# A hybrid decoder layer on one Trainium2 core: the norm gains loaded by themselves, the first weights loaded over two queues and cast by VectorE, the first sums for the down weights put behind the first plain chunk, and cached keys loaded ahead of raw query weights

## The chip, the cores and the metric

The kernel runs on one core of a Trainium2 chip. The core has TensorE (PE, matrix products into PSUM), VectorE (DVE), ScalarE (ACT), GpSimd (POOL) and SyncE (SP, which here only issues DMAs); ACT and POOL issue DMAs as well. The metric is the device time of one execution in microseconds (us). Three runs of the kernel before took 1117.34, 1118.7 and 1119.95 us; their median, 1118.7 us, is the time before.

## What is computed

One layer for 512 prompt positions and 8 x 8 sample positions that use the same weights (576 columns in all), with model width 1024, feed-forward width 2816, and 256 memory tokens in 4 heads of 256:

```
def swiglu(x, w_gate, w_up, w_down):
    return (jax.nn.silu(x @ w_gate) * (x @ w_up)) @ w_down

def layer_forward(x, conv_buf, lru_h, pool_buf, mem_k, mem_v, pos0, p):
    x = x + 0.5 * swiglu(rmsnorm(x, p['ffn1_norm']), p['ffn1_w_gate'], p['ffn1_w_up'], p['ffn1_w_down'])
    h = rmsnorm(x, p['mix_norm'])
    proj = h @ p['w_in']
...
    x = x + jnp.concatenate([y_lru, y_pool], axis=-1) @ p['w_out']
    x = x + cross_attend(rmsnorm(x, p['xattn_norm']), mem_k, mem_v, p['xattn_wq'], p['xattn_wo'])
    x = x + 0.5 * swiglu(rmsnorm(x, p['ffn2_norm']), p['ffn2_w_gate'], p['ffn2_w_up'], p['ffn2_w_down'])
    return x, conv_buf, lru_h, pool_buf
```

`rmsnorm(x, g)` is x times the reciprocal root of its mean square plus 1e-6, times the gain g. A last rmsnorm follows the layer. The prompt attends over keys and values made from `mem_prompt`, the samples over cached ones.

## The kernel before

**Operands.** Everything is float32. An operand is split into a high part of type float32r and the float32r remainder (`split`, L186): ACT makes the high part (the cast of L192, or L196 where a scale is applied) and DVE subtracts it (L195, L197). A product of two operands is three matmuls: high x high, high x low, low x high. x lies in SBUF with the model width along 128 partitions in 8 blocks k = 0 to 7 and 576 columns, in two halves of 288.

**Feed-forward.** Both feed-forward blocks run through one function, `ffn` (FFN1 with `head` set, FFN2 without). The width 2816 is 22 chunks of 128. FFN1 does chunks 0, 1 and 2 plainly: gate and up, 8 blocks k of 6 matmul pairs. `std_out` (L410) scales them by the row factor, applies Silu and multiplies. The other chunks (f = 3 to 21 in FFN1, f = 2 to 21 in FFN2, 39 in all) use seven products of half size in place of eight, with the weights' sums E, F, G, H beside the blocks 11, 12 and 22. The loop L806 to L880 writes one chunk: products 11, E, (22 and the rest of the chunk before), F, G, 12, H; between them stand preparations of the next chunks' weights (`prepare_e`, `prepare_g`, `prepare_h`, `prepare_22`, `sum_eh`) and, by `fill`, steps of the down projection of earlier chunks. `sum_eh` (L450) adds two weight blocks on DVE (L453) and starts a POOL DMA that adds a third from memory (L456). `prepare_g` adds the others (L471, L472). `prepare_22` casts and splits block 22 (128x512): the cast to tile `wh` on ACT and its remainder `wl` on DVE. The copy `u` of the U product (L852) stands in program order just ahead of `prepare_22`.

**Down projection.** `quick` (L633) does four chunks at a time in the same seven-product form, on PSUM tiles dU, dC, dA and dD. Its weights come from raw tiles `td` and `t` (SP DMAs L594, L600), with sums on DVE (L612, L614, L615, L623) in `ensure` and splits to `dh` and `dl`. ACT scales results out of PSUM (`take`, L642); POOL DMAs add them onto x.

**Head.** ACT issues the load of all constants (`cst`, 99 columns, L108); DVE negates two gains (L127, `neg`); a dummy activation loads the Sqrt table (L135); PE runs six warm matmuls (L141). Then SP loads, for k = 0 to 7, x[k] (L707), and, for even k, two blocks each of the gate and up weights of chunk 0 (L710, `wr`). For each k ACT and DVE split x[k] with the negated gain into `n1h` and `n1l` (`HalfNorm.split`, L330), for even k the weights into `wh` and `wl`, and PE does chunk 0's 12 matmuls of this k. `sums(p)` (L332) makes sums of the normed x on ACT and DVE for the seven-product form (tiles `t_ph`, `t_pl`). The row factor of FFN1's norm (L735 to L745) comes from squares of a second, row-wise copy of x (`xs`, L740, L741), Sqrt (L742) and a few small DVE steps (L285 to L289); PE spreads it over the partitions (the moves, L758 to L761) and ACT copies it to `rstd_n` (L764). `std_out(0)` then reads it (L416).

**Queries.** In the cross-attention `query(p)`, p = 0 to 3, makes queries of a pair of blocks by the same seven products. `load_q` loads raw query weights (`q`, L1333), `prepare_q` makes sums of them (on POOL for p > 0: L1344 to L1350) and splits them. `load_keys` loads cached keys (`ck`, L1317) and `sample_scores` multiplies them with the samples' queries on PE (tile `ss`). Raw weights and keys share six buffers of 512 KB (the tag `wr`): a load waits on SP until its buffer is free, and the loads queued behind it wait with it.

**Order.** `mm` chains every matmul of the feed-forward and query phases to the one before, so PE's order is that of the program. The order of DVE, ACT, POOL and SP is made by a scheduler from the program order, the dependences and a few hand-set "after" edges (`after_`, L142: an order on one engine, no wait). The edges touched here are `first[0]`, behind which casts of weights are held (L192), `row_done`, the last step of the row factor, and `out_[0]`, the last copy out of PSUM in the chunk loop.

## Time and profile before

| what | value |
|---|---|
| median of three runs | 1118.7 us (1117.34 to 1119.95) |
| the profiled execution's own time | 1118.21 us |
| its span on the core | 1116.1 us |
| busy time, share of the span | PE 99%, DVE 79%, ACT 62%, POOL 19% |
| matmuls | 8396 |
| DMA | 181.19 MB, mean 162 GB/s |
| granted TensorE clock | 0.999 |

The span is the time from the core's first instruction to its last; 2.1 us of the execution lie outside it. A row of the timeline gives start, duration, engine, line, operation, output and inputs, how many equal instructions in a row it stands for, and in brackets how long the engine was idle before and what ended that. SPq and ACTq rows are DMA issues, and their duration runs from the first issue to the end of the last.

### The profile page before, as it was taken

What the parts mean: (1) busy time and instruction counts of PE and PEld (TensorE: products, weight loads), DVE (VectorE), ACT (ScalarE), POOL (GpSimd) and SP (SyncE); (2) the same over time, 40 slices, a digit from 0 to 9 for tenths busy, and PEclk for the clock granted to TensorE, in tenths of its full rate; (3) what the DMA queues carried; (4) which work ended last, traced back from release to release, by engine and by line L of the source; (5) the groups of instructions that cost most, each with busy time, mean ns of one, the idle gap of its engine ahead of it and who ended that gap; (6) DMA issues with size and microseconds to landing.
All of it is one profiled execution on the core that took longest, in us unless ns stands there. A gap on an engine that the chain in (4) does not pass through costs nothing.

```text
span 1116.1 us, 22006 instructions
## 1 busy us (share of the span) xinstructions
PE 1101.8 (99%) x8396; PEld 1081.6 (97%) x8396; DVE 882.5 (79%) x1580; ACT 689.2 (62%) x1293; POOL 212.5 (19%) x248
## 2 busy tenths in 40 slices
PE   8999999999999999999999999999999999999997
PEld 8999999999999999999988879999999999999997
DVE  7899888889866878979865666779888888787755
ACT  8566666676664645786743555446666666666554
POOL 0012222221221034422131000000222122222211
PEclk9999999999999999999999999999999999999999
DMA  9457777776766655577557952233786877877652
GB/s 313 127 131 178 157 153 169 169 169 149 170 138 144 188 158 130 125 210 169 158 179 275 323 204 83 76 99 82 161 184 149 187 171 159 188 158 169 134 122 85
DMA packets 95577, 181.19 MB, mean 162 GB/s; under 512 B 10032, under 2 KB 47920, under 8 KB 95344
## 3 DMA queue, kind: packets, MB, share of 16 engines
q1 hardware_dynamic: 61328, 125.73, 35.3%
q0 software_dynamic: 31472, 51.65, 28.3%
q10 hardware_dynamic: 2672, 2.41, 0.6%
q8 instruction: 65, 1.06, 0.4%
q14 instruction: 40, 0.33, 0.1%
HBM read 141.92 MB, written 13.20 MB: 139 GB/s over the span
## 4 chain that ended last, share of the span: by engine, by line
PE 92%; issue 3%; DMA 2%; DVE 1%; ACT 1%; POOL 0%; SPq 0%; POOLq 0%; DVEq 0%; ACTq 0%
PE pu L149 23%; PE pc L149 11%; PE dU L149 9%; PE pa L149 5%; PE xo L149 5%; PE wo L149 5%; PE pd L149 4%; PE pg L149 3%; PE in_l L149 2%; PE in_p L149 2%; PE in_g L149 2%; PE dA L149 2%; PE dC L149 2%; PE dD L149 2%; PE k L149 2%
## 5 line engine op out<-in xcount | busy, mean ns | idle before, releaser
L456 POOL DMA_DIRECT2D r<-f_gu x39 | 34.9, 894 | 361.8 <-DVE r L453 197.7
L192 ACT CAST dh<-td 128x512 fp32r<-128x512 f32 x96 | 59.3, 617 | 31.2 <-PE dA L149 10.0
L149 PE MATMUL dU<-ph,dh 128*128 128x288 f32 x256 | 75.8, 296 | 1.4 <-ACT add L642 1.4
L149 PE MATMUL dU<-ph,dl 128*128 128x288 f32 x256 | 75.4, 295 | 0.0
L149 PE MATMUL dU<-pl,dh 128*128 128x288 f32 x256 | 75.4, 295 | 0.0
L195 DVE TENSOR_TENSOR dl<-td,dh 128x512 fp32r<-128x512 f32 x96 | 64.6, 685 | 10.2 <-ACT dh L192 10.1
L195 DVE TENSOR_TENSOR wl_e<-r,wh_e 128x1024 fp32r<-128x1024 f32 x39 | 47.7, 1222 | 28.4 <-ACT wh_e L192 28.4
L658 POOL DMA_DIRECT2D x<-add_e x32 | 38.9, 1215 | 144.2 <-ACT add_e L642 46.6
L192 ACT CAST wh_g<-r 128x1024 fp32r<-128x1024 f32 x39 | 41.0, 1051 | 27.0 <-PE pc L149 13.2
L685 POOL DMA_DIRECT2D x<-add x32 | 31.1, 971 | 137.8 <-ACT add L642 93.2
L149 PEld LDWEIGHTS dU<-ph,dh 128*128 128x128 f32 x256 | 48.1, 188 | 2.1 <-ACT add L642 2.1
L195 DVE TENSOR_TENSOR wl_h<-r,wh_h 128x1024 fp32r<-128x1024 f32 x39 | 47.6, 1219 | 3.0 <-ACT wh_h L192 3.0
L149 PEld LDWEIGHTS dU<-ph,dl 128*128 128x128 f32 x256 | 48.1, 188 | 0.0
L149 PEld LDWEIGHTS dU<-pl,dh 128*128 128x128 f32 x256 | 48.1, 188 | 0.0
L195 DVE TENSOR_TENSOR wl_g<-r,wh_g 128x1024 fp32r<-128x1024 f32 x39 | 47.6, 1221 | 0.3 <-ACT wh_g L192 0.3
L192 ACT CAST wh_h<-r 128x1024 fp32r<-128x1024 f32 x39 | 40.9, 1048 | 10.3 <-PE pu L149 7.2
L192 ACT CAST wh_e<-r 128x1024 fp32r<-128x1024 f32 x39 | 41.1, 1053 | 0.6 <-PE pg L149 0.6
L866 ACT ACTIVATE g<-g 128x576 f32<-128x576 f32 x39 | 26.6, 683 | 23.9 <-DVE g L865 22.3
L692 POOL DMA_DIRECT2D x<-add x32 | 37.0, 1156 | 1.0 <-ACT add L642 0.8
L192 ACT CAST ph<-g 128x576 fp32r<-128x576 f32 (+1 forms) x39 | 22.9, 588 | 18.6 <-DVE g L572 10.5
L831 ACT COPY e<-pc 128x288 f32<-128x288 f32 x39 | 15.6, 401 | 29.2 <-PE pc L149 28.2
L642 ACT ACTIVATE add<-dU 128x288 f32<-128x288 f32 x64 | 26.2, 409 | 11.6 <-PE dU L149 11.6
(656 smaller groups left out, 4649.0 us busy)
## 6 DMA issues: line engine op xcount, KB each, us to landing
x<-add POOLq DMA_DIRECT2D x80, 288.0 KB, 5.6
r<-f_gu SPq DMA_DIRECT2D x39, 512.0 KB, 4.0
r<-f_gu SPq DMA_DIRECT2D x78, 256.0 KB, 3.4
td<-f_d SPq DMA_DIRECT2D x80, 128.0 KB, 5.2
r<-f_gu POOLq DMA_DIRECT2D x39, 256.0 KB, 4.5
x<-add_e POOLq DMA_DIRECT2D x32, 288.0 KB, 4.7
dsum<-f_d POOLq DMA_DIRECT2D x32, 256.0 KB, 5.0
ck<-ck SPq DMA_DIRECT2D x16, 512.0 KB, 4.9
```

The lines of the kernel that those rows point to most:

```text
L149: i = te.matmul(*args, **kw)
L192: i = cast[0] = s.copy(hi, src)
L195: return v.tensor_tensor(out=lo, in0=src, in1=f(hi), op=ALU.subtract)
L456: nc.gpsimd.dma_start(r0[:, 0], wgu[f - plain, :, 3], accum_op=ALU.add)
L642: taken[0] = s.activation(dst, src, AF.Copy, scale=0.5 * sign)
L658: nc.gpsimd.dma_start(x[:, j:j + 2, HT:], t, accum_op=ALU.add)
L685: nc.gpsimd.dma_start(x[:, 2 * (i % NQ), :], t, accum_op=ALU.add)
L692: nc.gpsimd.dma_start(x[:, 2 * (i % NQ) + 1, :], t, accum_op=ALU.add)
L831: out_[0] = s.copy(e1, C)
L866: silu = s.activation(g, g, AF.Silu, scale=-1.0)
```

## The change

1. The constants' first 48 columns (all norm gains) are loaded alone at the start; the other 51 later. The first negation is only that of FFN1's gain, and FFN2's comes later. The dummy activation moves behind ACT's DMA issues. There are seven warm matmuls.
2. The up weights of k = 0 and 1 are loaded on ACT's queue. x[0] is split in two halves of 288 columns, DVE casts the two weight tiles of k = 0 and 1, and chunk 0's matmuls of k = 0 run in another order (all that need only high parts first).
3. The first DVE step of `sums(0)` stands behind the split of x[2].
4. The cast of the third plain chunk's gate weights is held behind the row factor's Sqrt in place of the copies of the spread factor, and its panel is loaded earlier in program order.
5. The weight sum of `sum_eh` for chunk 4 and the first two sums of `ensure` stand behind `plain_done`, the last DVE step of `std_out(0)`; before, one of them stood behind `row_done`.
6. In all 39 chunks the ACT cast of block 22 stands behind the copy `u`.
7. In `query(p)` for p > 0, the keys 2p - 2 are loaded where the raw query weights p + 2 were, and those where the keys were.

```diff
-WARM = 6
+WARM = 7
...
-    nc.scalar.dma_start(cst, a["consts"])
+    nc.scalar.dma_start(cst[:, :NGAIN], a["consts"][:, :NGAIN])
...
-    negate("g1", "g2")
+    negate("g1")
-    s.activation(rows.tile([P, T], F32, tag="acc", bufs=1, name="table")[:, :1], ones, AF.Sqrt)
...
-            split(hi, lo, halves(x[:, j, :]), ncol(self.gain, j))
-
-        def sums(self, p, t):
+            if j or self.acc is not None:
+                return split(hi, lo, halves(x[:, j, :]), ncol(self.gain, j))
+            else:
+                for h in range(2):
+                    split(hi[:, h, :], lo[:, h, :], x[:, j, h * HT:(h + 1) * HT], ncol(self.gain, j))
+
+        def sums(self, p, t, behind=None):
...
-            v.scalar_tensor_tensor(out=t1, in0=x11, scalar=ncol(self.gain, c1), in1=b12, op0=ALU.mult, op1=ALU.add)
+            i = v.scalar_tensor_tensor(out=t1, in0=x11, scalar=ncol(self.gain, c1), in1=b12, op0=ALU.mult, op1=ALU.add)
+            if behind is not None:
+                after_(i, behind)
...
-                if head and f == plain:
-                    after_(i, row_done)
+                if head and f < plain + 2:
+                    after_(i, plain_done if f > plain else row_done)
...
-                        v.tensor_add(slot(i, 3), slot(i, 0), slot(i, 1))
-                        e = v.tensor_add(slot(i, 0), slot(i, 0), draw[i])
+                        two = (v.tensor_add(slot(i, 3), slot(i, 0), slot(i, 1)),
+                               v.tensor_add(slot(i, 0), slot(i, 0), draw[i]))
                         if i == 0:
-                            after_(e, row_done)
+                            for e in two:
+                                after_(e, plain_done)
...
+            def load_w(queue, i, k):
+                queue.dma_start(ws[i][0][:, k:k + 2, :], wstd[0, i, :, k:k + 2, :])
+
+            load_w(nc.scalar, 1, 0)
             for k in range(DC):
                 nc.sync.dma_start(x[:, k, :], a["xT"][:, k, :])
-                if k % 2 == 0:
+                if k == 0:
+                    load_w(nc.sync, 0, 0)
+                elif k % 2 == 0:
                     for i in range(2):
-                        nc.sync.dma_start(ws[i][0][:, k:k + 2, :], wstd[0, i, :, k:k + 2, :])
+                        load_w(nc.sync, i, k)
+            s.activation(rows.tile([P, T], F32, tag="acc", bufs=1, name="table")[:, :1], ones, AF.Sqrt)
+            nc.scalar.dma_start(cst[:, NGAIN:], a["consts"][:, NGAIN:])
+            negate("g2")
             for k in range(DC):
-                n.split(k)
-                if k % 2 == 0:
+                if k == 0:
+                    for w, hi, _ in ws:
+                        v.tensor_copy(hi[:, :2, :], w[:, :2, :])
+                done = n.split(k)
+                if k == 2:
+                    second = done
+                if k == 0:
+                    for w, hi, lo in ws:
+                        v.tensor_tensor(out=lo[:, :2, :], in0=w[:, :2, :], in1=hi[:, :2, :].bitcast(F32), op=ALU.subtract)
+                elif k % 2 == 0:
                     for w, hi, lo in ws:
                         split(hi[:, k:k + 2, :], lo[:, k:k + 2, :], w[:, k:k + 2, :])
+                if k == 0:
+                    for i, qw, qx in ((0, 0, 0), (1, 0, 0), (0, 1, 0), (0, 0, 1), (1, 0, 1), (1, 1, 0)):
+                        for h, o in enumerate(cols(ps0[i])):
+                            mm(o, lhsT=ws[i][1 + qw][:, 0, :], rhs=n.part(qx, 0, N11 + h), start=qw + qx == 0, stop=False)
+                    continue
...
-                n.sums(i, ts[i // 2][:, i % 2])
+                n.sums(i, ts[i // 2][:, i % 2], None if i else second)
...
-            s.activation(y, ms, AF.Sqrt, scale=1.0 / (DC * P), bias=eps)
+            first[0] = s.activation(y, ms, AF.Sqrt, scale=1.0 / (DC * P), bias=eps)
...
+        if head:
+            w2 = panel(wstd[2, 0], DC, P, "s", load_behind=squares_in)
+            first[0] = None
...
-        std_out(0, *ps0)
+        plain_done = std_out(0, *ps0)
...
-            w = panel(wstd[2, 0], DC, P, "s", load_behind=squares_in)
+            w = w2
...
             prepare_22(f)
+            after_(cast[0], out_[0])
...
-            load_q(p + 2)
+            if p:
+                load_keys(2 * p - 2)
+            else:
+                load_q(2)
...
-                load_keys(2 * p - 2)
+                load_q(p + 2)
```

How the order of the engines changes at three places. First DVE from the last step of the row factor to the end of the first plain chunk, before (`wl_s` is the low part of the third plain chunk's gate weights, L416 and L418 scale chunk 0, `td` and L453 are the moved sums):

```order
L289 SCALAR_TENSOR_TENSOR rf_n_311<-rf_n_310,rf_n_311 128x5
L453 TENSOR_TENSOR r_455<-r_453 128x512
L416 TENSOR_TENSOR e<-pg_115,rstd_n_402 128x288
L416 TENSOR_TENSOR e<-pg_116,rstd_n_402 128x288
L416 TENSOR_TENSOR e<-pg_119,rstd_n_402 128x288
L416 TENSOR_TENSOR e<-pg_120,rstd_n_402 128x288
L195 TENSOR_TENSOR wl_s<-wr_s,wh_s 128x1024
L614 TENSOR_TENSOR td<-td 128x256
L453 TENSOR_TENSOR r_584<-r_582 128x512
L418 TENSOR_TENSOR e<-e,rstd_n_402 128x576 x2
```

The same stretch of DVE in the changed kernel, whose lines have other numbers (L287 is the old L289, L458 the old L453, L193 the old L195, L420 and L422 the old L416 and L418):

```order
L287 SCALAR_TENSOR_TENSOR rf_n_315<-rf_n_314,rf_n_315 128x5
L458 TENSOR_TENSOR r_459<-r_457 128x512
L193 TENSOR_TENSOR wl_s<-wr_s,wh_s 128x1024
L420 TENSOR_TENSOR e<-pg_113,rstd_n_412 128x288
L420 TENSOR_TENSOR e<-pg_114,rstd_n_412 128x288
L420 TENSOR_TENSOR e<-pg_117,rstd_n_412 128x288
L420 TENSOR_TENSOR e<-pg_118,rstd_n_412 128x288
L193 TENSOR_TENSOR n1l_102<-t_pl,n1h_100 128x864
L366 SCALAR_TENSOR_TENSOR t_pl<-x,cst,n1h_100 128x288
L422 TENSOR_TENSOR e<-e,rstd_n_412 128x576 x2
```

The step `wl_s` has moved ahead of the four L416 steps; the `td` sum and the second L453 sum have left this stretch, and the split of `sums(3)` (`n1l`) and a step of `last_sum` (L366, the old L362) have come forward into it.

Next DVE in the chunk loop, where it waits for the down weights `td` around 184 us of the trace, before (`wl_1538` is the low part of block 22, L471 and L472 are the sums of `prepare_g`):

```order
L614 TENSOR_TENSOR td<-td 128x256
L615 TENSOR_TENSOR td<-td,t_1451 128x256
L195 TENSOR_TENSOR wl_e<-r_1162,wh_e 128x1024
L804 TENSOR_TENSOR g<-pu,g 128x288
L195 TENSOR_TENSOR wl_1538<-r_1078,wh_1537 128x512
L195 TENSOR_TENSOR dl_1569<-t_1254,dh_1568 128x256
L471 TENSOR_TENSOR r_1162<-r_1162 128x512
L472 TENSOR_TENSOR r_1162<-r_1162,r_1244 128x512
```

And the same rows in the changed kernel (L619, L620, L835, L476 and L477 are the old L614, L615, L804, L471 and L472):

```order
L619 TENSOR_TENSOR td<-td 128x256
L620 TENSOR_TENSOR td<-td,t_1455 128x256
L193 TENSOR_TENSOR wl_e<-r_1166,wh_e 128x1024
L835 TENSOR_TENSOR g<-pu,g 128x288
L193 TENSOR_TENSOR dl_1573<-t_1258,dh_1572 128x256
L476 TENSOR_TENSOR r_1166<-r_1166 128x512
L477 TENSOR_TENSOR r_1166<-r_1166,r_1248 128x512
L193 TENSOR_TENSOR wl_1542<-r_1082,wh_1541 128x512
```

The low part of block 22 now stands behind the two sums of `prepare_g`.

Last, SP's loads in the query loop, before (q_2 and q_3 are raw query weights of p = 2 and 3; the first pair of `ck` tiles holds the keys j = 1, the second the keys 0, the third the keys 3):

```order
L1333 DMA q_2_7074<-wqs 128x1024
L1333 DMA q_2_7075<-wqs 128x1024
L1317 DMA ck_7174<-ck 128x1024
L1317 DMA ck_7175<-ck 128x1024
L1333 DMA q_3_7218<-wqs 128x1024
L1333 DMA q_3_7219<-wqs 128x1024
L1317 DMA ck_7256<-ck 128x1024
L1317 DMA ck_7257<-ck 128x1024
```

The changed kernel (L1365 is the old L1333, L1349 the old L1317):

```order
L1365 DMA q_2_7078<-wqs 128x1024
L1365 DMA q_2_7079<-wqs 128x1024
L1349 DMA ck_7178<-ck 128x1024
L1349 DMA ck_7179<-ck 128x1024
L1349 DMA ck_7222<-ck 128x1024
L1349 DMA ck_7223<-ck 128x1024
L1365 DMA q_3_7260<-wqs 128x1024
L1365 DMA q_3_7261<-wqs 128x1024
```

The keys 0 have moved ahead of the raw query weights of p = 3, and take the two buffers that those took.

More of the change, by code (lines that the diff above doesn't have):

```diff
@@ L61 @@
 NCONST = _n
+NGAIN = _C["cw"]
 NSTATE = LC * NB * 3 + LC * NB + LC * NB * PW
@@ L419, in std_out @@
             for p, q in pieces(pu, e):
-                v.scalar_tensor_tensor(out=q, in0=p, scalar=-1.0, in1=q, op0=ALU.mult, op1=ALU.mult)
+                out = v.scalar_tensor_tensor(out=q, in0=p, scalar=-1.0, in1=q, op0=ALU.mult, op1=ALU.mult)
             raw[i] = e
+            return out
         raws, W = {}, {}
```

## The prediction

> **What bounds the kernel now.** I read the waits of TensorE first, then busy time by stage, then the timeline at each wait. The waits (engine, line and tile, what it waited for, total us, times, longest):
>
> ```profile
> PE ss L149 <- DMA ck<-ck: 1.6, 2, 1.1
> PE warm L149 <- POOL ident masks.py:199: 1.4, 1, 1.4
> PE dU L149 <- ACT add L642: 1.4, 3, 0.7
> PE pg L149 <- ACT wh L192: 1.3, 1, 1.3
> PE pu L149 <- ACT u L852: 1.2, 1, 1.2
> PE pg L149 <- DVE n1l L197: 0.8, 2, 0.4
> ```
>
> Busy time by stage (window, length, then PE, PEld, DVE, ACT and POOL, the granted clock, DMA share, GB/s):
>
> ```profile
> 0.00:20.00 20.00, 16.59 (x106) 15.34 (x107) 14.62 (x32) 15.89 (x29) 0.70 (x6) 1.00 0.90 313
> ...
> 60.00:80.00 20.00, 18.83 (x141) 18.52 (x140) 19.86 (x36) 15.09 (x30) 2.98 (x3) 1.00 0.51 124
> ...
> 180.00:200.00 20.00, 19.47 (x147) 19.25 (x147) 14.46 (x27) 12.42 (x25) 4.64 (x5) 1.00 0.79 180
> ...
> 560.00:580.00 20.00, 18.43 (x150) 17.00 (x148) 13.93 (x20) 8.65 (x14) 8.53 (x7) 1.00 0.41 142
> ...
> 740.00:1080.00 340.00, 340.00 (x2573) 340.00 (x2572) 272.44 (x474) 215.40 (x432) 70.66 (x74) 1.00 0.70 156
> ```
>
> TensorE is the bound: all of FFN2 (740 to 1080) has no gap at all. No matmul is removed, so only its gaps can be won: 3.4 us at the head (20.00 - 16.59), 1.2 near 70 us, 0.5 near 190, 1.6 near 578. The edits aim at these; what they can win together is some 5 us of 1118, under half a per cent, and anything that opens a gap in a full stage is a loss. About 0.2% (2.2 us) is what a measurement of this kernel tells from no change.
>
> **The head.** The timeline (start, us, engine, line, operation, idle before):
>
> ```profile
> 3.07 0.91 SPq L710 DMA_DIRECT2D wr<-f_s  x2
> ...
> 4.22 0.80 SPq L707 DMA_DIRECT2D x<-xT  x2
> 4.22 0.24 DVE L127 TENSOR_SCALAR neg<-cst 128x8 f32<-128x8 f32 x2 [1.40 <-DMA cst<-consts]
> 4.43 0.77 ACT L196 ACTIVATE n1h<-x,neg 128x576 fp32r<-128x576 f32 x1 [1.74 <-DVE neg L127]
> 5.11 0.39 ACT L192 CAST wh<-wr 128x256 fp32r<-128x256 f32 x1
> ...
> 5.55 0.53 PE L149 MATMUL pg<-n1h,wh 128*128 128x288 f32 x2 [1.26 <-ACT wh L192]
> ...
> 5.97 0.76 DVE L195 TENSOR_TENSOR wl<-wr,wh 128x256 fp32r<-128x256 f32 x2
> ...
> 6.88 0.78 ACT L196 ACTIVATE n1h<-x,neg 128x576 fp32r<-128x576 f32 x1 [0.65 <-DMA x<-xT]
> ...
> 7.71 0.54 PE L149 MATMUL pg<-n1h,wh 128*128 128x288 f32 x2
> ```
>
> Before, the constants land at 4.22, then ACT makes `n1h` (0.77) and the cast (0.39) one after the other, and PE starts at 5.55. After, even with the gains no earlier, ACT makes half of x[0] (0.4 to 0.5, half of 0.77 and something fixed, an estimate) while DVE makes the cast. How long a DVE cast of 128x256 takes no row shows; the nearest are 0.38, each of the two `wl` rows (0.76), and 0.39, ACT's cast: I take 0.4 each. From 4.4 that puts the first matmul at about 4.9, 0.6 us earlier. The seventh warm matmul fits into the 1.26 us in which PE stood idle before it. The 12 matmuls of k = 0 then wait for x[1] as before, so what counts is x[1]: it is issued at 4.22, behind two weight loads that begin at 3.07 and take 0.91. With one of them on ACT's queue it can go after the first, at 3.07 + 0.46 = 3.53: 0.69 earlier. ACT then waited 0.65 for it, so that much is real. I take **-0.7**. Ends: 0, if bytes and not issue slots bound the loads (DMA is busy at 0.90 in this window); -1.4, if the moved `sums(0)` step also frees DVE for the two `n1l` waits (0.8 in the table of waits). DVE's new work, two casts and one more half split, about 0.9 us, stands against that second gain, so I take nothing for it. The table load that moves behind ACT's DMA issues has cover, since ACT was done at 2.69 (4.43 - 1.74); if it came over 1.7 us later, it would push `n1h` and the start by the excess. The rest of the constants and FFN2's negation are read long after the head: nothing.
>
> The Trainium skill, "DMA: Bandwidth & Descriptors", section "Queues, rings and completion order", says that the queues of SP and ACT are rings on the same 16 engines, which alternate between them packet by packet. The 128 KB moved to ACT's queue would then still stand beside x[1], and the gain would be the 0.7 less their transfer, by the 313 GB/s of the row above 0.4 us: 0.3 in all. The 0.90 of the row speaks for it as an average; the 0.65 us in which ACT waited for x[1] doesn't tell the two apart. This is the first rival below.
>
> **The row factor and the stop near 70 us.** DVE at the first plain chunk, and the chain that stops PE later:
>
> ```profile
> 27.90 0.17 DVE L289 SCALAR_TENSOR_TENSOR rf_n<-rf_n,rf_n 128x5 f32<-128x5 f32 x1
> ...
> 29.76 0.32 ACT L764 COPY rstd_n<-pg 128x192 f32<-128x192 f32 x1 [2.52 <-PE pg L149]
> ...
> 30.61 1.77 DVE L416 TENSOR_TENSOR e<-pg,rstd_n 128x288 f32<-128x288 f32 x4 [1.88 <-ACT rstd_n L764]
> 32.30 1.22 DVE L195 TENSOR_TENSOR wl_s<-wr_s,wh_s 128x1024 fp32r<-128x1024 f32 x1
> ...
> 51.32 1.05 ACT L192 CAST wh_e<-r 128x1024 fp32r<-128x1024 f32 x1
> ...
> 69.25 0.44 DVE L572 TENSOR_TENSOR g<-g,t 128x288 f32<-128x288 f32 x1
> ...
> 69.73 0.43 ACT L192 CAST ph<-g 128x288 fp32r<-128x288 f32 x1
> ...
> 70.07 0.39 ACT L852 COPY u<-pu 128x288 f32<-128x288 f32 x1
> ...
> 70.51 0.40 PE L149 MATMUL pu<-n1h,wh_h 128*128 128x288 f32 x1 [1.17 <-ACT u L852]
> ```
>
> The copy `u` is late because ACT first casts `ph`, which waits for DVE's step L572, and DVE is behind: in 60 to 80 us it is busy 19.86 of 20. But at 28.7 it stood idle for 1.88 us, until the row factor was spread. Edit 4 puts `wl_s` (1.22, some 1.13 from start to start, estimate) into that gap. Edit 5 only reorders the sums ahead of L572: the moved `td` and L453 steps are paid later but still before it. The POOL DMA behind the moved chunk-4 sum goes out some 5 us later for it (eight DVE steps, an estimate); ACT's cast that reads its result runs only at 51.32, so nothing; without that cover the E product of chunk 4 would wait. Edit 6 moves chunk 3's `wl` behind L572, and an L453 sum of the same size comes ahead of it in exchange. So L572 comes 1.13 us earlier, and PE's idle 1.17 falls to about nothing: **-1.2**. Ends: 0, if another step of that crowded stretch is then late, and -1.3, with the slow start of the matmul after a wait. Also at risk is the row factor: DVE ends it at 28.07 and ACT's copies come at 29.76, so 1.4 us or so of slack, less the 0.7 by which PE comes earlier; I price it at nothing.
>
> **The chunk loops.** Block 22's cast and low part move in 39 chunks. Two places of the same kind, near 190 and 259 us, and one at 160:
>
> ```profile
> 159.88 0.40 PE L149 MATMUL dU<-ph,dh 128*128 128x288 f32 x1 [0.17 <-ACT add L642]
> ...
> 184.67 0.43 DVE L614 TENSOR_TENSOR td<-td 128x256 f32<-128x256 f32 x1 [4.94 <-DMA td<-f_d]
> ...
> 186.97 0.68 DVE L195 TENSOR_TENSOR wl<-r,wh 128x512 fp32r<-128x512 f32 x1
> ...
> 187.57 0.42 DVE L195 TENSOR_TENSOR dl<-t,dh 128x256 fp32r<-128x256 f32 x1
> ...
> 190.82 0.40 PE L149 MATMUL dU<-ph,dh 128*128 128x288 f32 x1 [0.53 <-ACT add L642]
> ...
> 258.92 0.40 PE L149 MATMUL dU<-ph,dh 128*128 128x288 f32 x1 [0.67 <-ACT add L642]
> ```
>
> At 184.67 DVE has waited 4.94 us for down weights; behind it `wl`, then L472, then ACT's `wh_g`, and behind that on ACT the `add` that PE needs at 190.82. After, `wl` stands behind L472: 0.60 (187.57 - 186.97) earlier, at both places: -0.5 and -0.6. Against it: near 154 us, and in two later groups of four chunks, DVE waits for `td` too, but before the change `wl` ran ahead of that wait; now it runs behind it, and the chain that ends at 159.88, already late by 0.17, comes up to 0.5 later: three times +0.35 to +0.5. Together **0**, ends -1.1 and +1.5. FFN2 has no gap, and the new orders there move steps within stretches in which DVE does not wait: 0, with the third rival as its upper end.
>
> **The keys.** SP's issues (the second row begins with the keys 0), and PE's wait:
>
> ```profile
> 569.27 1.86 SPq L1333 DMA_DIRECT2D q<-wqs  x2
> 571.24 9.87 SPq L1317 DMA_DIRECT2D ck<-ck  x4
> ...
> 578.85 0.64 PE L149 MATMUL ss<-ck,z_acc 128*32 128x256 f32 x8 [1.05 <-DMA ck<-ck]
> ```
>
> And from the list of DMA issues (count, KB each, median us from issue to landing):
>
> ```profile
> ck<-ck SPq DMA_DIRECT2D x16, 512.0 KB, 4.9
> ```
>
> PE waits 1.05 us for the first of the two key loads, and again for the second, 1.6 in all. They are issued from 571.24 on, into buffers that came free last; a key load takes 4.9 us (median). After, they go into the buffers of the raw weights, from 569.27 on: the last of the two begins at the latest at 571.13 (569.27 + 1.86), and landing it 4.9 later, at 576.0, is 1.8 us ahead of the 577.8 (578.85 - 1.05) at which PE asks. **-1.5**; ends -1.6, and 0 if these loads take as long as the second did before, some 8 us. The raw weights then come two us later; they are used on POOL, which waits anyway, and by PE a whole query later: nothing.
>
> **Sum.** -0.7 - 1.2 + 0 - 1.5 = -3.4 us. On the profiled execution (1118.21, of it 1116.1 the span) that gives 1114.8. The median shown is 1118.7, so on its scale **1115.3**.
>
> **Rivals.**
> First, *bytes bound the first loads*: x[1] and the rest land no earlier than the bytes ahead of them allow, the head gives 0.3 or nothing. For it: DMA share 0.90. Against: ACT's wait of 0.65 came right after SP's issue gap. -0.1 - 1.2 - 1.5 = -2.8: 1115.9.
> Second, *the stop near 70 us is handed on*: with DVE at 19.86 of 20, another step there (the low parts of the down weights, which PE reads at 64 us, or the `td` sums that moved behind the plain chunk) is late in its place, and the `td` pattern costs its +0.5 net. -0.7 - 0 + 0.5 - 1.5 = -1.7: 1117.0. For it: the crowded stretch; against: the work taken out of it is 1.13 us and nothing is added.
> Third, *slower: the cast of block 22 is late in every chunk*. The groups of ACT show
>
> ```profile
> L192 ACT CAST wh<-r 128x512 fp32r<-128x512 f32 x39 | 24.2, 620 | 7.9 <-PE pu L149 4.0 <-PE pc L149 3.7
> ```
>
> Before, ACT did this cast while it waited for PE's U product; after, it waits idle, copies `u`, and then casts, so 0.5 us or so of ACT's work moves behind each wait, and the down projection's copies with it. If that reaches PE for 0.15 us in each of 39 chunks, it costs 5.9: -3.4 + 5.9 = +2.5, 1121.2. Slower begins at 0.15 us a chunk. Against: ACT is busy 215 of 340 us in FFN2, and `u` itself comes earlier.
> Fourth, *the keys do not land earlier*: the buffers they take come free only as DVE and POOL finish with the old weights, and two loads at once slow each other. -0.7 - 1.2 = -1.9: 1116.8.
>
> **How the numbers follow.** The forecast 0.48 (its own range 1113.4 to 1116.4, from the ends of its terms without the zeros of the rivals), bytes 0.15, handed on 0.17, keys 0.10, slower 0.10. The first two are faster by over 2.2 us, with a little of the keys: 0.64. The second rival and the rest of the fourth lie within: 0.26. Slower: 0.10. The range leaves out the slower case and the outermost of the gains: it reaches from 1113.0 (-5.7: -1.4 - 1.3 - 1.1 - 1.6, and a little for what the terms miss) to 1118.3 (the second rival with 1.3 for three more `td` waits).
>
> **What would show it.** Right: first real matmul near 4.9 us, x[1]'s split near 6.2, no PE wait on `u` near 70, none on `ck` near 577, waits on `add` moved from 190 and 259 to 160, 227 and 297. Wrong: PE waits in FFN2 on `add` or on `pu` (the third rival), a new wait at the moves near 29 us, x[1] still at 6.9, or a PE gap at 60 to 70 us on another tile.

## The result, and the profile after

The changed kernel is slower: the median of six runs is 1124.66 us (1123.40 to 1127.51), against 1118.10 for six runs of the kernel before (1116.58 to 1119.95), a ratio of 1.0065 with an interval of 1.0054 to 1.0075. That is 6.6 us more where 3.4 less were forecast, and outside the range. The profiled execution took 1123.40 us, with a span of 1121.4; the span of before was 1116.1.

In the code after, the line numbers are a little higher: `mm` L147, the split L190 to L197, `add` L648, `dD` L670, `u` L883, the first down sums L619 and L620 (L614 and L615 before), `prepare_g` L476 and L477 (L471 and L472), and the difference `g<-g,t` that `ph` is cast from L577 (L572).

The waits of TensorE after (engine, line and tile, what it waited for, total us, times, longest):

```profile
PE dU L147 <- ACT add L648: 6.1, 5, 1.9
PE pu L147 <- ACT u L883: 2.0, 3, 0.8
...
PE dU L147 <- ACT dD L670: 1.3, 1, 1.3
PE pg L147 <- ACT n1h L194: 0.6, 1, 0.6
```

Against the table of before, the waits on `ck`, on the first `wh` and on the long `u` near 70 us are gone as predicted. But the wait on `add` has grown from 1.4 to 6.1 us, and `u` and `dD` stop TensorE at new places. The busy time by stage says where (window, length, PE, PEld, DVE, ACT, POOL, clock, DMA share, GB/s):

```profile
0.00:20.00 20.00, 17.92 (x118) 17.03 (x118) 15.09 (x34) 16.11 (x28) 0.71 (x6) 1.00 0.90 302
...
60.00:80.00 20.00, 19.76 (x150) 19.52 (x149) 19.80 (x36) 14.21 (x29) 3.89 (x4) 1.00 0.61 153
80.00:180.00 100.00, 95.33 (x715) 94.42 (x714) 82.27 (x152) 60.83 (x127) 21.59 (x22) 1.00 0.71 156
180.00:200.00 20.00, 19.08 (x144) 18.85 (x143) 15.62 (x30) 12.33 (x27) 5.69 (x6) 1.00 0.72 160
200.00:240.00 40.00, 37.32 (x280) 36.85 (x279) 33.03 (x62) 23.94 (x50) 7.97 (x9) 1.00 0.63 144
...
560.00:580.00 20.00, 20.00 (x163) 19.25 (x162) 13.83 (x21) 10.80 (x19) 4.14 (x3) 1.00 0.40 131
740.00:1080.00 340.00, 340.00 (x2573) 340.00 (x2573) 275.13 (x477) 210.43 (x426) 68.97 (x72) 1.00 0.68 154
```

The head gained 1.3 us of busy time (16.59 to 17.92), the stretch near 70 us 0.9 (18.83 to 19.76), the keys 1.6 (18.43 to 20.00), and FFN2 is still full. All of the loss lies in FFN1's chunk loop. Between 80 and 180 us TensorE was busy 99.83 before and 95.33 now. The windows from 80 to 360 us lose 8.0 us in all (278.53 busy of 280 before, 270.56 after). TensorE's idle time in the whole span went from 14.3 (1116.1 - 1101.8 busy) to 18.4 (1121.4 - 1103.0). The other 1.2 us of the longer span is longer busy time. At least part of that is the first matmul after each stop, which takes 0.40 in place of 0.29; two of the matmuls are new warm ones.

The first stop shows the mechanism. This is the timeline of DVE after (start, us, engine, line, operation, idle before and its cause):

```profile
100.40 0.43 DVE L619 TENSOR_TENSOR td<-td 128x256 f32<-128x256 f32 x1 [3.47 <-DMA td<-f_d]
100.74 0.75 DVE L195 SCALAR_TENSOR_TENSOR pl<-g,ph 128x576 fp32r<-128x576 f32 x1
101.41 0.69 DVE L477 TENSOR_TENSOR r<-r,r 128x512 f32<-128x512 f32 x1
102.01 0.45 DVE L577 TENSOR_TENSOR g<-g,t 128x288 f32<-128x288 f32 x1
```

ACT and TensorE behind it, after:

```profile
102.50 0.43 ACT L190 CAST ph<-g 128x288 fp32r<-128x288 f32 x1 [4.55 <-DVE g L577]
102.84 0.39 ACT L883 COPY u<-pu 128x288 f32<-128x288 f32 x1
103.13 0.62 ACT L190 CAST wh<-r 128x512 fp32r<-128x512 f32 x1
103.65 0.40 ACT L670 COPY dD<-dU 128x288 f32<-128x288 f32 x1
...
104.10 0.40 PE L147 MATMUL dU<-ph,dh 128*128 128x288 f32 x1 [1.30 <-ACT dD L670]
```

The same DVE steps before:

```profile
100.57 0.45 DVE L572 TENSOR_TENSOR g<-g,t 128x288 f32<-128x288 f32 x1
...
102.52 0.42 DVE L614 TENSOR_TENSOR td<-td 128x256 f32<-128x256 f32 x1
```

Before, the step that makes `g` ran first, and the sum of the down weights came 1.95 us after it and waited for nothing. Now the sum stands ahead, finds its weights not landed, and holds DVE for 3.47 us. `g`, and on ACT `ph`, `u`, `wh` and `dD`, wait behind it, and TensorE stops for 1.30 us on `dD`.

It goes on in the next block of down weights, since the held DVE steps also free the buffers of `td` later (SP waits for DVE's `dl`, which reads them). The SP queue issues that block's loads at 110.32 before:

```profile
110.32 2.00 SPq L594 DMA_DIRECT2D td<-f_d  x3
```

and after at 111.58, although TensorE had come to 80 us with a lead of some two us from the earlier edits:

```profile
111.58 1.74 SPq L599 DMA_DIRECT2D td<-f_d  x3
...
117.79 0.42 DVE L619 TENSOR_TENSOR td<-td 128x256 f32<-128x256 f32 x1 [5.03 <-DMA td<-f_d]
...
121.93 1.05 ACT L190 CAST wh_g<-r 128x1024 fp32r<-128x1024 f32 x1 [2.60 <-DVE r L477]
122.89 0.40 ACT L648 ACTIVATE add<-dU 128x288 f32<-128x288 f32 x1
123.33 0.40 PE L147 MATMUL dU<-ph,dh 128*128 128x288 f32 x1 [0.72 <-ACT add L648]
```

The two longest stops, 1.92 us at 163.02 and 1.83 at 234.12, are of another kind. The first:

```profile
163.02 0.40 PE L147 MATMUL dU<-ph,dh 128*128 128x288 f32 x1 [1.92 <-ACT add L648]
```

Ahead of it the sum stands behind the `g` step of its chunk (L567, at 152.74) and waits 3.64 us for its weights, and the low part `wl` (157.62) runs only then. These are two of the three places at which the prediction expected a loss, of 0.35 to 0.5 us each.

In all, DVE waits 35.8 us in 13 places for `td` after, and 26.3 us in nine before. How much of such a wait reaches TensorE depends on what stands behind it.

One correction: the second pair of orders in the section on the change, said to be near 184 us, shows the rows of the group of chunks before (near 117 us). At 184 us the same steps stand in the same order.

### The profile page after: what moved, and what is told of

Same layout as the page of the kernel before. It is cut to its first block, busy times and chain, and to the rows that moved or that the text cites. A ratio compares the mean times of both kernels' runs of the same rounds, so it can differ in the third digit from the quotient of the medians.

```text
span 1121.4 us, 21942 instructions
## 1 busy us (share of the span) xinstructions
PE 1103.0 (98%) x8398; PEld 1082.3 (97%) x8398; DVE 884.6 (79%) x1583; ACT 681.8 (61%) x1292; POOL 210.9 (19%) x248
## 4 chain that ended last, share of the span: by engine, by line
PE 77%; DVE 9%; DMA 7%; issue 4%; ACT 2%; SPq 0%; POOL 0%; POOLq 0%; DVEq 0%; ACTq 0%
PE pu L147 17%; PE pc L147 8%; PE dU L147 6%; DMA td<-f_d 5%; PE xo L147 5%; PE wo L147 5%; PE pd L147 4%; PE pa L147 4%; PE pg L147 3%; PE in_l L147 2%; PE in_p L147 2%; PE in_g L147 2%; PE k L147 2%; PE v L1497 2%; PE dA L147 2%
## 5 line engine op out<-in xcount | busy, mean ns | idle before, releaser
L147 PE MATMUL dU<-ph,dh 128*128 128x288 f32 x256 | 76.1, 297 | 7.4 <-ACT add L648 6.1
L190 ACT CAST dh<-td 128x512 fp32r<-128x512 f32 x96 | 59.2, 618 | 34.9 <-PE dA L147 9.1
L147 PE MATMUL dU<-ph,dl 128*128 128x288 f32 x256 | 75.5, 295 | 0.2 <-DVE dl L193 0.2
L147 PE MATMUL dU<-pl,dh 128*128 128x288 f32 x256 | 75.4, 295 | 0.0
L193 DVE TENSOR_TENSOR dl<-td,dh 128x512 fp32r<-128x512 f32 x96 | 64.5, 685 | 7.3 <-ACT dh L190 6.8
L193 DVE TENSOR_TENSOR wl_e<-r,wh_e 128x1024 fp32r<-128x1024 f32 x39 | 47.7, 1222 | 23.6 <-ACT wh_e L190 23.6
L664 POOL DMA_DIRECT2D x<-add_e x32 | 38.9, 1215 | 145.6 <-ACT dh L190 49.5
L147 PEld LDWEIGHTS dU<-ph,dh 128*128 128x128 f32 x256 | 48.1, 188 | 8.8 <-ACT add L648 7.3
L190 ACT CAST wh_g<-r 128x1024 fp32r<-128x1024 f32 x39 | 41.1, 1053 | 24.8 <-DVE r L477 11.3
L193 DVE TENSOR_TENSOR wl_h<-r,wh_h 128x1024 fp32r<-128x1024 f32 x39 | 47.5, 1219 | 3.3 <-ACT wh_h L190 3.3
L147 PEld LDWEIGHTS dU<-ph,dl 128*128 128x128 f32 x256 | 48.2, 188 | 0.5 <-DVE dl L193 0.5
L147 PEld LDWEIGHTS dU<-pl,dh 128*128 128x128 f32 x256 | 48.1, 188 | 0.0
L193 DVE TENSOR_TENSOR wl_g<-r,wh_g 128x1024 fp32r<-128x1024 f32 x39 | 47.5, 1219 | 0.3 <-ACT wh_g L190 0.3
L190 ACT CAST wh_h<-r 128x1024 fp32r<-128x1024 f32 x39 | 40.8, 1046 | 9.0 <-PE pu L147 5.9
L190 ACT CAST wh_e<-r 128x1024 fp32r<-128x1024 f32 x39 | 41.1, 1054 | 0.6 <-PE pg L147 0.6
L190 ACT CAST ph<-g 128x576 fp32r<-128x576 f32 (+1 forms) x39 | 22.9, 588 | 27.8 <-DVE g L577 16.8
L193 DVE TENSOR_TENSOR wl<-r,wh 128x512 fp32r<-128x512 f32 x39 | 26.9, 691 | 11.6 <-ACT wh L190 9.2
L619 DVE TENSOR_TENSOR td<-td 128x256 f32<-128x256 f32 x16 | 6.8, 424 | 35.8 <-DMA td<-f_d 35.8
```

The costliest lines, as they stand in the source:

```text
L147: i = te.matmul(*args, **kw)
L190: i = cast[0] = s.copy(hi, src)
L193: return v.tensor_tensor(out=lo, in0=src, in1=f(hi), op=ALU.subtract)
L619: two = (v.tensor_add(slot(i, 3), slot(i, 0), slot(i, 1)), v.tensor_add(slot(i, 0), slot(i, 0), draw[i]))
L664: nc.gpsimd.dma_start(x[:, j:j + 2, HT:], t, accum_op=ALU.add)
```

## The experiments

The theory after this reading: edit 6 alone causes the loss, by the place it gives the first sums of the down weights on DVE, and the other edits together do about what was forecast. The rival: edit 6 costs by its own order on ACT (the cast of block 22 behind `u`), as the prediction's third rival had it; or edits 4 and 5, which also move such sums, share in the loss. Each ratio below is against the kernel before, run beside it (medians 1117.63 to 1117.81).

**All edits but 6.**

```diff
-            after_(cast[0], out_[0])
```

> The changed kernel without edit 6 (block 22's cast is no longer held behind the copy u). Theory A (order): edit 6 alone makes the scheduler put the first td sum ahead of DVE's step L577, so DVE waits for a load with work behind it that TensorE needs; without it the waits on add, dD and u in the chunk loop of FFN1 fall from 9.4 us to about 1.5, and the time is 1114 to 1115.5 (ratio to before 0.996 to 0.998). Theory B (phase): the earlier head makes TensorE run into loads that come no earlier; then the waits stay and the time is above 1121. Theory C (cast): the cast itself, late on ACT, costs the time; same number as A here.

Measured: 1114.50 us, ratio 0.9971 (0.9960 to 0.9981), 3.2 us faster than before. TensorE's stages:

```profile
80.00:180.00 100.00, 99.94 (x755) 99.70 (x755) 86.57 (x159) 66.77 (x138) 24.25 (x25) 1.00 0.76 169
180.00:200.00 20.00, 19.64 (x148) 19.41 (x148) 17.02 (x32) 11.54 (x22) 3.89 (x4) 1.00 0.74 168
200.00:240.00 40.00, 40.00 (x304) 40.00 (x303) 36.38 (x69) 26.86 (x57) 9.07 (x9) 1.00 0.72 158
```

The new stops are gone. What stays are the two old ones, 0.36 us at 188.29 and 0.39 at 255.73 (`PE dU <- ACT add`, 0.8 in all).

**Edit 6 alone on the kernel before** (the same line added).

> The kernel before with edit 6 alone. Theory A: all of the loss and none of the gains, about 8 us: 1126 to 1128 (ratio 1.007 to 1.009), with stops at 102, 122, 137, 160, 193, 208, 232, 264 and 280 us as in the changed kernel, some 1.5 us later each. Theory B: no loss without the earlier head, 1118 (ratio 0.999 to 1.001). Theory C: as A.

Measured: 1128.76 us, ratio 1.0100 (1.0085 to 1.0115), 11.1 us slower than before and a little above what was expected. Its DVE:

```profile
102.95 0.43 DVE L614 TENSOR_TENSOR td<-td 128x256 f32<-128x256 f32 x1 [3.51 <-DMA td<-f_d]
...
104.56 0.45 DVE L572 TENSOR_TENSOR g<-g,t 128x288 f32<-128x288 f32 x1
```

The edge on ACT alone, one line, puts the sum on DVE ahead of `g`, with the same hold (3.51). With the run before it, edit 6 is shown to be the whole cause of the loss.

**After, with the first sums held behind `g`.** Edit 6 stays, and only the place of the sums is undone:

```diff
-            v.tensor_sub(b21, b21, t2[p])
+            last_b[0] = v.tensor_sub(b21, b21, t2[p])
...
-                        if i == 0:
-                            for e in two:
+                        for e in two:
+                            if i == 0:
                                 after_(e, plain_done)
+                            elif last_b[0] is not None:
+                                after_(e, last_b[0])
```

> The changed kernel, edit 6 kept, with the first two td sums of each down block held behind the last build_b subtraction (L577) written before them. Theory A: the stops at 102, 137, 160, 208, 232 and 280 us shrink to 0.5 or less, and the time is 1114.5 to 1118. Theory C: the cast still stands behind u, so the time stays at 1123 to 1126. Theory B: the same, above 1121.

Measured: 1116.66 us (twelve runs, 1113.11 to 1119.82), ratio 0.9995 (0.9983 to 1.0007): 8.0 us less than the changed kernel. So the order on ACT, which this kernel keeps, isn't what costs that. Three stops stay: 1.33 us at 158.72, 0.31 at 189.44 and 1.33 at 227.60. The first and the last are longer than the 0.5 expected at most. The first:

```profile
152.52 0.42 DVE L622 TENSOR_TENSOR td<-td 128x256 f32<-128x256 f32 x1 [4.17 <-DMA td<-f_d]
...
153.32 0.68 DVE L193 TENSOR_TENSOR wl<-r,wh 128x512 fp32r<-128x512 f32 x1
...
156.25 0.45 DVE L902 TENSOR_TENSOR g<-pa,rstd_n 128x288 f32<-128x288 f32 x1
...
158.72 0.41 PE L147 MATMUL dU<-ph,dh 128*128 128x288 f32 x1 [1.33 <-ACT add L653]
```

The stops near 158 and 227 us are at two of the three places for which the prediction forecast a loss (160, 227 and 297): there `wl` stands behind the sum's wait, and all that follows comes later. The third place shows none. The one near 189 us is the old stop of before near 190.

**After, with the first sums held behind `g` and behind the last low part of block 22.** The run before with one edge more:

```diff
-            split(*w, raw22.pop(f))
+            last_b.append(split(*w, raw22.pop(f)))
...
+                                after_(e, last_b[-1])
```

> The changed kernel with edit 6, the first td sums held behind both the build_b subtraction and the last written low part of block 22. Theory A: with both steps of DVE ahead of the td wait again, the two stops of 1.5 us near 157 and 226 us that were left go too, though the cast still stands behind u: 1113.5 to 1115.5. Theory C: those two stops are the cast's own and stay: 1116.5.

Measured: 1112.73 us (1111.11 to 1113.18), ratio 0.9954 (0.9942 to 0.9967), the fastest of all that compute the whole layer, 4.9 us under the kernel before. Its waits on DVE for `td`, and two stages of TensorE:

```profile
DVE td L622 <- DMA td<-f_d: 6.1, 3, 2.6
```

```profile
80.00:180.00 100.00, 100.00 (x758) 100.00 (x757) 88.39 (x162) 66.53 (x138) 24.24 (x25) 1.00 0.77 168
180.00:200.00 20.00, 20.00 (x153) 20.00 (x152) 18.41 (x33) 11.86 (x25) 3.89 (x4) 1.00 0.86 186
```

With the sums late in DVE's queue, 35.8 us of waits become 6.1, since DVE does other work while the weights land, and the stops near 190 and 259 us that edit 6 was to remove are gone too. Not all of that need be the order's work. In this profile TensorE's first matmuls run slower (two in a row take 0.68 us up to 10 us, where they mostly take 0.43 in the run before), and it reaches the chunk loop 1.3 us later: the same `dU` matmul starts at 79.09, and at 77.83 in the run before. At 158 us `add` is then ready only 0.3 us ahead of the matmul that needs it. The gain of 3.9 us over the run before rests on the times of five and twelve runs; that the stop would stay away with TensorE as early as there is not shown.

**After, without the loads that the sums wait for.** In FFN1 the raw down weights are loaded for the first block alone, so the others are summed from what lies in the buffers:

```diff
-                        nc.sync.dma_start(slot(i, k), wq[g, q, :, k])
+                        if i == 0:
+                            nc.sync.dma_start(slot(i, k), wq[g, q, :, k])
```

> The changed kernel with edit 6 kept; the raw down weights of FFN1 are loaded for the first block only, so that the td sums of the later blocks have nothing to wait for (the later down projections are made from stale weights: part of the loads is left out). Theory A (order): with no load to wait for, a td sum ahead of L577 costs DVE 0.4 us and no more; the stops at 102 to 280 us go but for single ones under 0.5, the waits of DVE on td (35.8 us) fall to about nothing, and the time is 1113 to 1116. Theory C (cast): the ACT cast behind u is as late as before, the waits on add and u stay at 6 us or more, 1121 to 1125.

Measured: 1112.94 us, ratio 0.9956 (0.9944 to 0.9969); TensorE is busy 100.00 of 100 between 80 and 180 us. The order of the changed kernel, sums ahead of `g` and all, costs nothing that shows once there is no load to wait for, and ends where the run before ends. So the price is the waits for `td`. This run also moves fewer bytes (148 GB/s between 80 and 180 us, 156 in the changed kernel), but the run before moves them all and ends at the same time. TensorE starts as slowly here as there; at 158 us `add` is ready 1.7 us ahead of its matmul, more than that delay.

**All edits but 6, with the first sums put ahead of `g` by hand.** ACT's order is that of the kernel without edit 6, and in chunks 6, 10 and 14 the sum is written earlier and `g` is held behind it:

```diff
-            v.tensor_sub(b21, b21, t2[p])
+            b = v.tensor_sub(b21, b21, t2[p])
+            if hold:
+                after_(b, hold.pop())
...
+                if head and f in (6, 10, 14):
+                    ensure(made[0] + 1)
+                    hold.append(first_sums((made[0] + 3) // 4)[0])
```

> The changed kernel without edit 6, with the two first td sums of three down blocks (3, 7 and 11) put ahead of the build_b subtraction (L577) of chunks 6, 10 and 14 by hand, where edit 6 had made the scheduler put them; ACT's order is that of the run without edit 6. Theory A (order): the position alone costs the time; a new stop on dD, add or u near 102, 170 and 237 us of 1 to 1.5 us each, 1116.5 to 1119 against 1114.5. Theory C (cast): no stop comes back, 1114 to 1115.

Measured: 1122.64 us, ratio 1.0042 (1.0029 to 1.0056), slower than before without edit 6. The size missed the expectation, upwards. Its DVE and SP:

```profile
101.32 0.43 DVE L613 TENSOR_TENSOR td<-td 128x256 f32<-128x256 f32 x1 [3.62 <-DMA td<-f_d]
...
112.17 1.73 SPq L601 DMA_DIRECT2D td<-f_d  x3
...
118.05 0.43 DVE L613 TENSOR_TENSOR td<-td 128x256 f32<-128x256 f32 x1 [4.71 <-DMA td<-f_d]
```

The stop at the hold itself is only 0.52 us (at 104.88). Behind the late loads the next block stops TensorE for 1.58 us at 124.20, and in the later groups for 2.25 at 193.97 and 2.53 at 263.74. With neither edit 6 nor this order, the loads go out 3.5 us earlier (1.1 of it is a wait on the row factor that this profile has and the other has not):

```profile
108.68 1.73 SPq L599 DMA_DIRECT2D td<-f_d  x3
```

I had priced the hold and not the loads that it delays.

**All edits but 6, with `wl` late in two chunks.** An attempt to get edit 6's gain at 190 and 259 us alone: in chunks 11 and 15 the low part of block 22 is written behind `prepare_g`'s sums.

```diff
-            split(*w, raw22.pop(f))
+            if head and f in (11, 15):
+                src = raw22.pop(f)
+                cast[0] = s.copy(w[0], src)
+                late_.append((w, src, out_[0]))
+            else:
+                split(*w, raw22.pop(f))
```

> The changed kernel without edit 6, and in chunks 11 and 15 alone the low part of block 22 written behind prepare_g's sums (the cast on ACT stays where it was). The stops at 187.6 and 255.1 us (0.5 each) hang on those sums; if the low part ahead of them is what makes them late, both go: 1113.5, 1 us under the run without edit 6 (ratio 0.9955 to 0.997). Rival: the wait for the td load ahead of both sets the stop, and it stays.

Measured: 1116.88 us, ratio 0.9995 (0.9986 to 1.0003): a miss. The two stops fell to 0.17 and 0, and two new ones came:

```profile
PE pu L147 <- ACT u L888: 1.7, 2, 0.9
```

They lie at 204 and 272 us, in the next block of down weights. Ahead of the first, DVE's order is that of the run without edit 6, but the first sum runs at 199.11 and not at 197.43; its loads went out at 192.22 and not at 191.05. A low part moved within one block was paid in the next, by later loads; TensorE itself was 0.6 us later there, and the share of each is not tested.

**Edits 1 to 3 alone** (the head; the rest of the diff undone).

```diff
-            first[0] = s.activation(y, ms, AF.Sqrt, scale=1.0 / (DC * P), bias=eps)
+            s.activation(y, ms, AF.Sqrt, scale=1.0 / (DC * P), bias=eps)
...
-            after_(cast[0], out_[0])
```

> Edits 1 to 3 alone (constants, first loads and casts, first sums). From the two traces the first 20 us lose 2.1 us where they lost 3.4: 1.3 us less, 1116.8 (ratio 0.9983 to 0.9995). Theory B, that the earlier head alone upsets the chunk loop: 1119 or more.

Measured: 1118.24 us (1115.93 to 1121.11), ratio 1.0010 (1.0000 to 1.0020): not the gain that was expected. The first 20 us gain 1.8 (18.41 busy), and the next 20 give 1.2 back:

```profile
PE pg L147 <- DVE rf_n L287: 1.0, 1, 1.0
```

TensorE comes earlier to the spread of the row factor and waits for it.

**Edits 4 and 5 alone on the kernel before.**

```diff
+            first[0] = s.activation(y, ms, AF.Sqrt, scale=1.0 / (DC * P), bias=eps)
...
+                            for e in two:
+                                after_(e, plain_done)
```

> Edits 4 and 5 alone (third plain panel's cast behind the Sqrt, first sums behind the first plain chunk). By the prediction the stop near 70 us (1.2) goes and nothing takes its place: 1116.5 (ratio 0.9985 to 0.9995). Rival: without the earlier head the row factor has more slack, but the stop is handed on to another wait at 60 to 70 us, and the time is that of before, 1117.5.

Measured: 1117.86 us, ratio 0.9998 (0.9988 to 1.0008). In the window from 60 to 80 us TensorE is busy 19.76, as in the whole change, so the stop near 70 us is gone (a wait of 0.2 on `dl` near 64 us is new). The time does not show the gain that was expected: the interval runs from -1.3 to +0.9 us. These edits alone leave the sums of the loop behind `g`.

**Edit 7 alone on the kernel before.**

```diff
-            load_q(p + 2)
+            if p:
+                load_keys(2 * p - 2)
+            else:
+                load_q(2)
...
-                load_keys(2 * p - 2)
+                load_q(p + 2)
```

> Edit 7 alone (keys ahead of raw query weights). By the prediction the wait on ck (1.6) goes and nothing comes in its place: 1116.3 (ratio 0.9982 to 0.9992). Rival (keys): they land no earlier, 1117.5 or more.

Measured: 1116.11 us, ratio 0.9987 (0.9978 to 0.9996): 1.5 us faster, with no wait on `ck` and 20.00 of 20 in the window from 560 to 580.

**Edits 1 to 5** (the whole change without 6 and 7).

```diff
-            after_(cast[0], out_[0])
...
-                load_keys(2 * p - 2)
+                load_q(p + 2)
```

> Edits 1 to 5. Between this and the run with edits 1 to 5 and 7 lies the keys' term alone: by the prediction 1.5 us, so 1116.0 (ratio 0.998 to 0.9990), with the wait on ck (1.6) back and no wait on the row factor at 28 us. Rival: the keys' wait is partly made up elsewhere, 1114.5 to 1115.

Measured: 1116.18 us, ratio 0.9988 (0.9979 to 0.9998). The run without edit 6 alone, which adds edit 7 to this, is 1.7 us faster, where 1.5 was forecast for the keys. The wait on the row factor, not expected here, is in its profile too (1.0; the profiled execution, 1119.45 us, is the slowest of the twelve). Its ACT:

```profile
25.13 1.06 ACT L769 ACTIVATE xs_pl<-xs_pl 128x1024 f32<-128x1024 f32 x1 [0.68 <-DMA xs_pl<-xs]
...
27.60 0.30 ACT L770 ACTIVATE rf_n<-ms_n,ones 128x5 f32<-128x5 f32 x1
```

The second of these steps without edit 6 alone:

```profile
26.59 0.30 ACT L770 ACTIVATE rf_n<-ms_n,ones 128x5 f32<-128x5 f32 x1
```

Here ACT waited for the row-wise x, and the Sqrt came 1.0 us later. Of the nine profiles with edits 1 to 3, four show this wait (0.6 to 1.1 us) and five, the changed kernel among them, do not. The Sqrt comes at 26.59 to 27.74 in the nine; why it varies so is open.

## Why the prediction was wrong

**The step that failed** is the chunk loops: "Together **0**, ends -1.1 and +1.5". They cost 8.0 us of busy time net between 80 and 360 us. Two things were wrong in it.

The larger one was missing altogether. I followed `wl` past the sums that wait for down weights, and did not look at which other step those sums had passed. The change moved the first sum ahead of the `g` step, and by the trace of before that sum lay 1.95 us behind it and waited for nothing; its new place lies at a time at which the weights have not landed. (In two later blocks, at 200.42 and 268.12, the sum stood ahead of `g` before too, with waits of 1.15 and 0.76 us and no stop; new is the place in the blocks near 100, 134 and 172 us.) What this hoisting costs is 8.0 us: the changed kernel at 1124.66 against 1116.66 with the sums back behind `g`. By TensorE's idle time between 80 and 360 us in the two profiles it is 6.5 (9.4 against 3.0), so the size is known to a microsecond or two. Putting the sums there without edit 6 costs nearly as much: 1122.64 against 1114.50, 8.1 us, of which the wait on the row factor in that profile may be 1.1. Why an edge on ACT makes the scheduler place a DVE step otherwise is argued from the order alone: with the cast later, `wl` is no longer ready at that point, and the sum, ready by the scheduler's own reckoning, is taken in its stead. No run tests that.

The smaller one was mis-sized: `wl` behind the wait at 154 us and in two later groups, "three times +0.35 to +0.5", 1.1 to 1.5 in all. With the sums behind `g` two of the three places stop TensorE, for 1.33 us each, 2.7 in all; in the changed kernel these two stops are 1.92 and 1.83. The run without edit 6 shows where that comes from, since TensorE reaches the loop there as early as with the sums behind `g` (the `dU` matmul at 77.82 and 77.83) and does not stop near 158:

```profile
151.81 0.42 DVE L619 TENSOR_TENSOR td<-td 128x256 f32<-128x256 f32 x1 [2.84 <-DMA td<-f_d]
...
154.82 0.45 DVE L896 TENSOR_TENSOR g<-pa,rstd_n 128x288 f32<-128x288 f32 x1
```

With edit 6 the same two steps run at 152.52 and 156.25. So `g` is 1.43 us later. `wl` and what comes with it make 0.72 of that (`g` is 3.73 behind the sum in place of 3.01). The other 0.71 is the sum itself, whose weights land later; the issue of its three loads begins at the same time in both (145.49 and 145.46) and ends 0.5 later with edit 6. The prediction had 0.35 to 0.5 for the first part and nothing for the second, and why the loads come later is open.

What edit 6 was forecast to win, 0.5 and 0.6 near 190 and 259 us, came only in part by edit 6: without it the two stops are 0.36 and 0.39, and with it and the sums behind `g` 0.31 and none. With the sums behind `wl` as well, both are gone.

**The head**, -0.7 forecast. The spread row factor is copied at 28.63 (29.76 before), so the head brought 1.1 in the changed kernel, near the far end of its range; the 1.3 of busy time contain the seventh warm matmul. Not every execution gets this. Of the nine profiles with edits 1 to 3, three copy the factor at 28.5 to 28.6, four at 29.2 to 29.6, behind the wait on the row factor, and two at 29.7 to 29.8, where TensorE's first matmuls run at 0.68 us for two up to 9 or 10 us. Such slow first matmuls also come without the edits (up to 8.2 to 9.0 us in the runs of edit 6, of edits 4 and 5 and of edit 7 alone), and why is open. So busy time at the head says less than it seems to. The starts in the changed kernel:

```profile
1.67 0.90 SPq L717 DMA_DIRECT2D x<-xT  x2
...
4.55 0.24 DVE L128 TENSOR_SCALAR neg<-cst 128x8 f32<-128x8 f32 x2 [3.65 <-DMA cst<-consts]
...
4.87 0.55 DVE L729 CAST wh<-wr 128x256 fp32r<-128x256 f32 x2
...
5.35 0.83 PE L147 MATMUL pg<-n1h,wh 128*128 128x288 f32 x2 [0.62 <-ACT n1h L194]
...
6.05 0.76 ACT L194 ACTIVATE n1h<-x,neg 128x576 fp32r<-128x576 f32 x1
```

The working was wrong in its row. The SP row at 4.22 that I took for x[1] issues x[3] and x[4]; x[1] is the first of the pair at 2.12, and went out 0.45 us earlier (1.67). It was split 0.83 earlier, at 6.05 (6.2 forecast). That holds in every profile: 5.64 to 6.09 in the nine with edits 1 to 3, 6.82 to 7.39 in the four without. The gain is there, with a reason that was half right. In this profile the norm gains were there at 4.55 and not 4.22, so the first matmul came at 5.35, not 4.9; in six of the other eight it comes at 4.92 to 4.98, as forecast.

The rule on rings that alternate, weighed in the prediction (the Trainium skill, "DMA: Bandwidth & Descriptors", section "Queues, rings and completion order"), would have left 0.3 us. The run does not show that loss: x[1] was there 0.83 us earlier with the other queue's weights beside it. So the first rival is out.

The row factor was "at risk" and priced at nothing, with 1.4 us or so of slack. The slack was 1.1: DVE ended the factor at 28.07, and PE's moves began at 29.17, ahead of ACT's copies at 29.76. In the changed kernel 0.05 of it is left (27.89 against 27.94), which is just enough. In four of the nine profiles it is not, and the wait takes 0.6 to 1.1 us of the head's gain.

**The stop near 70 us**, -1.2 forecast: `g` comes at 66.95 (69.25 before), `u` at 67.78, TensorE does not wait there, and the moves of the row factor show no wait. A new wait of 0.24 on `dl` near 63 us leaves 0.9. The second rival named that tile at 64 us; it takes back a fifth of the gain, not all of it.

**The keys**, -1.5 forecast: 1.5 alone, 1.7 on top of edits 1 to 5, 1.6 by the window. In the changed kernel the loads start at 564.18 and the scores do not wait. The fourth rival is out.

**The third rival** had the sign and not the mechanism. The cast of block 22 is no cost in 39 chunks: FFN2, with 20 of them, is busy 340.00 of 340, and the kernel with edit 6 and the sums held is the fastest.

Without edit 6 the sum of the other terms, -0.7 - 1.2 - 1.5 = -3.4, was measured as -3.2 (1114.50 against 1117.66), the head's surplus standing against the smaller gain near 70 us. That the sum agrees so well is partly luck: measured alone, the three parts gave +0.6 (the head), 0.0 (edits 4 and 5) and -1.5 (the keys), -0.9 together, with intervals of about 1 us to each side.

## What to carry to other kernels

An "after" edge that costs no wait on its own engine can still reorder another engine. Compare the orders of every engine, and for each step that waits for a load list what it now stands ahead of, not only what has come behind it. Where a step must wait for a DMA on an engine that serves others in order, put it as late as its own reader allows: here two edges turned 35.8 us of such waits into 6.1, and a loss of 6.6 us into a gain of 4.9. A wait at the head of a queue also delays the freeing of buffers and so the next loads. Where only the sums were moved, that second round cost more than the first (1.58 us against 0.52); in the changed kernel it cost less (0.72 against 1.30).

## What the runs showed of the hardware

Loading half of the constants took no less time. The list of DMA issues (KB each, us from issue to landing), after:

```profile
cst<-consts ACTq DMA_DIRECT2D x1, 25.5 KB, 4.3
cst<-consts ACTq DMA_DIRECT2D x1, 24.0 KB, 3.8
```

and before:

```profile
cst<-consts ACTq DMA_DIRECT2D x1, 49.5 KB, 3.5
```

24 KB landed in 3.8 us and 49.5 KB in 3.5. Over the profiles it is 3.3 to 3.8 us for 24 KB (the nine with edit 1) and 3.4 to 3.8 for 49.5 KB (the four without). This agrees with the Trainium skill, "DMA: Bandwidth & Descriptors", section "Bandwidth", by which transfers under 64 KB are bound by their descriptors and not by their bytes. Its table's times are not comparable: they are busy spans of DMAs issued by GpSimd, and those here run from issue to landing.

A cast of 128x256 on DVE took 0.29 us (two in a row 0.55), not the 0.4 that I took from the subtraction of the same size (0.42 in this trace). The Trainium skill, "VectorE: DVE Perf Modes", section "The perf-mode tier table (the rule you actually need)", gives a copy of float32 in SBUF twice the rate of an operation with two tensors. The rows agree for a cast to float32r, once a fixed part is taken off: the subtraction of 128x512 takes 0.69, so 256 more columns cost 0.27 and the fixed part is 0.15 (an estimate); without it the cast takes 0.14 and the subtraction 0.27.
